# Weight ring of a mixture-of-experts layer: buffers laid out once, and the refill after the first round taken singly, into half a buffer

## Chip, cores and metric

The kernel runs on one core of a Trainium2 chip. The metric is the device time of one execution in microseconds (us); of several runs the median is given.

## The reference

One layer of an encoder on 512 tokens of width 1024, in float32. Three token mixers (neighbourhood attention, grouped-query attention, attention into 256 memory tokens) run on projections of the same input and are merged with gates; then comes a normalization, and then a feed-forward layer of 16 experts in which each expert chooses its 64 tokens:

```python
logits = jnp.einsum('btd,de->bte', x, w_router)
aff = jax.nn.softmax(logits, axis=-1)
gate, idx = lax.top_k(jnp.swapaxes(aff, 1, 2), cap)      # cap = 64
xs = x[bidx, idx]
h = jnp.einsum('becd,edf->becf', xs, w_gate_up)          # w_gate_up (16, 1024, 2048)
hg, hu = jnp.split(h, 2, axis=-1)
ye = jnp.einsum('becf,efd->becd', jax.nn.silu(hg) * hu, w_down)   # w_down (16, 1024, 1024)
...
return jnp.zeros_like(x).at[bidx, idx].add(ye)
```

A second normalization of `alpha * x + ffn` is the output. The experts' weights are 16 x 3 x 1024 x 1024 floats, 201 MB, and every one of them is needed.

## The kernel before

The program has two halves. In the first, TensorE works through the mixers' projections; their weights come through buffers of their own. In the second, the 16 experts follow one another. The instructions of each engine stand in the order in which the program writes them, and each engine waits for semaphores where it needs another's result.

The experts' weights are cut into 192 units of 128 rows by 2048 floats (1.05 MB, 8 KB in each of the 128 partitions). Expert `e` has eight units `("gu", e, k)` for the products `g` and `u` (function `gate_up`, line 1295) and four units `("dn", e, k)` for `y` (function `down`, line 1330; for the last expert `product`, line 1450). `_blocks` (lines 44 to 61) puts the units in the order of their use and deals them out in rounds to the twelve buffers of `RING`: ten hold a pair (16 KB in each partition), and `raw` and `VS` one unit. Three buffers serve only one or two rounds (`ROUNDS`), after which the kernel uses their space for results. The first round holds units 0 to 21.

The class `Ring` (lines 793 to 844) issues the transfers on SyncE's queue. `load` takes the next block, lays out a tile `w<number>` in its buffer and issues one DMA (line 817), or, for blocks that reach into the last `N_SINGLE` = 10 units, one for each unit (line 815). The first round is issued during the first half, as its buffers come free. After that `done`, which `gate_up`, `down` and `product` call behind the products of a unit, counts the units left in the block; when a block has been used up, the next block of the stream is issued. Since SyncE's queue keeps its order, an issue that waits holds those behind it. A DMA also waits until the eighth DMA before it has landed, since eight semaphores are taken in turn. In HBM the units lie in the order of the blocks (`_expert_rows`); the two units of a pair lie interleaved, so that a partition's 16 KB are one run.

While the tokens are being chosen the ring is full and no transfer is under way. Then `gather` collects the first two experts' tokens, and expert 0's eight `gu` units are used with a step of `gather` between them:

```python
if e == 0:
    for k in range(KD):
        gate_up(0, (k,))
        steps(g0)
```

Near the end, `ring.free_at_end` gives the tag of a buffer that no further block needs; its space takes parts of the sum `acc`.

Of the kernel before, what the change touches and what calls it, by code (L numbers as in the profile page):

```python
# [18 lines left out]
P = 128  # L19
D = 1024  # L20
# [11 lines left out]
RING = (("Q2", 2), ("Q1", 2), ("Q5", 2), ("Q7", 2), ("Q4", 2), ("Q3", 2), ("Q6", 2), ("raw", 1), ("Q9", 2), ("VS", 1),  # L32
        ("G1", 2), ("M", 2))
ROUNDS = {"raw": 1, "G1": 2, "VS": 2}
N_SINGLE = 10
X_SCALE = 1024.0
A_SCALE = 16384.0


def lead(e):  # L40
    return 2 if e == NEXP - 2 else 4


def _blocks():
    order = []
    for e in range(NEXP - 1):
        order += [("gu", e, k) for k in range(lead(e))]
        if e:
            order += [("dn", e - 1, k) for k in range(4)]
        order += [("gu", e, k) for k in range(lead(e), KD)]  # L50
    order += [("gu", NEXP - 1, k) for k in range(KD)]
    order += [("dn", e, k) for e in (NEXP - 2, NEXP - 1) for k in range(4)]
    blocks, i, r = [], 0, 0
    while i < len(order):
        for tag, n in RING:
            left = ROUNDS.get(tag, len(order)) - r
            if left > 0 and i < len(order):
                blocks.append((tag, n, order[i:i + n], i + n > len(order) - N_SINGLE, left > 1))
                i += n
        r += 1  # L60
    return blocks

# [2 lines left out]
def layer_kernel(ctx: ExitStack, tc: tile.TileContext, xt, xn, first0, wu, bgate, rpb, gains, wrt,  # L65
                 lnp, lnt, wx, csn, nmask, tri, iota, out, dbg=None):
    nc = tc.nc
# [12 lines left out]
    def R(tag, shape, name, dt=F32, bufs=None):  # L80
        return rp.tile(shape, dt, name=name, tag=tag, bufs=bufs)
# [55 lines left out]
    class Stream:  # L137
        AHEAD_DMA = 2

        def __init__(self):  # L140
            self.nd = 0
            self.ns = 0
            self.used = 0
            self.raw = {}
            self.hl = {}
# [121 lines left out]
    gT = cp.tile([P, KD], F32, name="gT")  # L267
    nc.gpsimd.tensor_scalar(gT, lnT[:, 0], 1.0 / X_SCALE, None, op0=ALU.mult)

# [523 lines left out]
    class Ring:  # L793
        def __init__(self):
            self.blocks = _blocks()
            self.at = {}
            self.row = [0]
            for b, (_, n, keys, _, _) in enumerate(self.blocks):
                self.row.append(self.row[-1] + P * n)
                for j, key in enumerate(keys):  # L800
                    self.at[key] = (b, j)
            self.n = 0
            self.left = [len(b[2]) for b in self.blocks]
            self.lent = len(RING)
            self.t = {}
            self.free_at_end = []

        def load(self):
            tag, n, keys, apart, _ = self.blocks[self.n]
            r0 = self.row[self.n]  # L810
            full = R(tag, [P, 2 * n, D], f"w{self.n}")
            src = wx[r0:r0 + P * len(keys)].rearrange("(p j) (h c) -> p (j h) c", j=len(keys), h=2)
            if apart:
                for j in range(len(keys)):
                    nc.sync.dma_start(full[:, 2 * j:2 * j + 2], src[:, 2 * j:2 * j + 2])
            else:
                nc.sync.dma_start(full[:, :2 * len(keys)], src)
            for j, key in enumerate(keys):
                t = [full[:, 2 * j + h] for h in range(2)]
                if key[0] == "dn" and key[1] == NEXP - 1:  # L820
                    t = [x.rearrange("p (c n) -> p c n", c=4) for x in t]
                self.t[key] = t
            self.n += 1

        def upto(self, n):
# [7 lines left out]
            return self.t.pop(key)  # L833

        def done(self, *key):
            b, _ = self.at[key]
            self.left[b] -= 1
            if self.left[b] == 0:
                tag, again = self.blocks[b][0], self.blocks[b][4]
                if again:  # L840
                    if self.lent >= len(self.blocks):
                        self.free_at_end.append(tag)
                    self.lent += 1
            self.upto(self.lent)

    ring = Ring()
    for i in range(4):
# [220 lines left out]
    def norm_cols(ms):  # L1068
        c = slice(ms[0], ms[-1] + 1)
        nc.gpsimd.tensor_scalar(r13[:, c], rs_y[:, c], X_SCALE, None, op0=ALU.mult)  # L1070
        for m in ms:
# [298 lines left out]
    def residual():  # L1370
        for h in range(2):
# [8 lines left out]
            for mp in range(2):  # L1380
                nc.vector.scalar_tensor_tensor(a[mp], a[mp], DN_ALPHA / X_SCALE, g, op0=ALU.mult, op1=ALU.mult)
                if mp == 0:
# [271 lines left out]
def _down_slots(w):  # L1654
    import numpy as np
    a = w.reshape(NEXP, 4, 2, 128, 1024).swapaxes(2, 3).reshape(NEXP, 4, 128, 2048).copy()
    a[-1] = w[-1].reshape(2, 4, 128, 4, 256).transpose(3, 2, 0, 1, 4).reshape(4, 128, 2048)
    return a


def _expert_rows(wgu, wdn):
    import numpy as np
    dn = _down_slots(wdn)
    unit = {"gu": lambda e, k: wgu[e, k * P:(k + 1) * P], "dn": lambda e, k: dn[e, k]}
    return np.concatenate([np.stack([unit[t](e, k) for t, e, k in keys], 1).reshape(-1, 2048) for _, _, keys, _, _ in _blocks()])


def _norm_rows(g1, b1, g2, b2):
# [17 lines left out]
def _prep(inp):  # L1686
# [51 lines left out]
    for ty in range(3):  # L1738
# [20 lines left out]
        "lnp": _norm_rows(*(np.asarray(inp[n])[0] for n in ("ln1_g", "ln1_b", "ln2_g", "ln2_b"))),  # L1759
        "lnt": np.stack([np.asarray(inp[n])[0].reshape(8, 128).T for n in ("ln1_g", "ln1_b")], 1),  # L1760
        "wx": _expert_rows(np.asarray(inp["w_gate_up"])[0], np.asarray(inp["w_down"])[0]),
        "csn": csn, "nmask": nmask, "tri": tri,
        "iota": np.broadcast_to(np.arange(1, 65, dtype=f), (128, 64)),
# [24 lines left out]
```

## Time and profile before

| what | value |
|---|---|
| median of 3 runs | 968.36 us (968.03 to 968.84) |
| the profiled execution | 967.9 us |
| its span in the profile | 966.1 us |
| TensorE busy in the span | 943.5 us (98%) |
| moved by DMA | 251.19 MB |
| ring DMAs by the page (2048 KB; 1024 KB) | 89; 14 |
| granted TensorE clock | 0.998 |

The profile is of one execution. Times in it count from the start of its span. TensorE's matmuls are pipelined and their ends are modelled, so that a share of 98% doesn't say that no matmul waited. PE is TensorE, ACT ScalarE, DVE VectorE, POOL GpSimd, SP SyncE; SPq is SyncE's sequencer, which issues the DMAs. `w<-in_wx` are the ring's transfers. A row of a window gives the busy time and the number of instructions of each engine, then the granted clock, the share of time in which the 16 DMA engines were busy, and the rate in GB/s.

### The profile page before, as it was taken

The numbers are of one execution on the slowest core, as the hardware profiler recorded it, in microseconds if no ns is written. First come the engines' busy times: TensorE is split into PE (matmuls) and PEld (weight loads), VectorE is DVE, ScalarE is ACT, GpSimd is POOL, SyncE is SP. The second block draws the span as 40 slices with busy tenths as digits, with TensorE's granted clock in tenths as the row PEclk, the third lists the DMA queues.
The fourth block names the chain that finished last, engine by engine and source line by source line (L and its number), as shares of the span: only waits on it lengthen the run. The fifth ranks groups of instructions, "written<-read, shape, count | busy, mean of one in ns | idle before, by whom it ended". The sixth has DMA issues, their size and how long they took to land.

```text
span 966.1 us, 13195 instructions
## 1 busy us (share of the span) xinstructions
PE 943.5 (98%) x5406; PEld 615.1 (64%) x5406; DVE 453.0 (47%) x851; ACT 277.2 (29%) x545; POOL 84.6 (9%) x98
## 2 busy tenths in 40 slices
PE   9999999999999999999999999999999999998996
PEld 9899878889888888887885333433343333532344
DVE  6347668874376566237464212653322222231426
ACT  5334454544354454323242111100010001100123
POOL 0102303000022231000023000000000000000003
PEclk9999999999999999999999999999999999999999
DMA  9321111211333322575919999999999999999992
GB/s 361 113 67 66 66 66 44 67 61 50 102 104 105 100 82 84 213 285 206 370 50 373 410 427 433 430 428 431 432 428 430 431 431 429 431 430 432 428 408 94
DMA packets 38329, 251.19 MB, mean 260 GB/s; under 512 B 12911, under 2 KB 13295, under 8 KB 24830
## 3 DMA queue, kind: packets, MB, share of 16 engines
q1 hardware_dynamic: 37550, 249.74, 63.9%
q8 instruction: 42, 0.69, 0.3%
q10 hardware_dynamic: 720, 0.62, 0.2%
q14 instruction: 17, 0.14, 0.0%
HBM read 247.46 MB, written 2.10 MB: 258 GB/s over the span
## 4 chain that ended last, share of the span: by engine, by line
PE 80%; DMA 10%; DVE 6%; ACT 1%; issue 1%; POOL 1%; DVEq 0%; POOLq 0%; ACTq 0%; SPq 0%
DMA w<-in_wx 10%; PE g L1295 10%; PE u L1295 9%; PE y L1330 8%; PE gate L274 4%; PE gate L275 4%; PE gate L276 4%; PE pr L274 2%; PE gy L649 2%; PE ga L1255 2%; PE pr L275 2%; PE pr L276 2%; PE nqk L274 2%; PE nqk L276 2%; PE nqk L275 2%; PE gt L636 1%
## 5 line engine op out<-in xcount | busy, mean ns | idle before, releaser
L1295 PE MATMUL g<-w,xs 128*64 128x512 f32 x512 | 135.1, 606 | 4.0 <-DMA w<-in_wx 3.9
L1295 PE MATMUL u<-w,xs 128*64 128x512 f32 x512 | 131.6, 592 | 0.0
L1330 PE MATMUL y<-w,hT 128*64 128x512 f32 x480 | 106.6, 594 | 3.4 <-DMA w<-in_wx 2.7
L93 DVE TENSOR_TENSOR y<-y,y 64x512 fp32r<-64x512 f32 x30 | 20.7, 689 | 134.5 <-ACT y L92 134.5
L1295 PEld LDWEIGHTS u<-w,xs 128*64 128x64 f32 x512 | 36.8, 137 | 73.1 <-issue 72.3
L92 ACT CAST y<-y 64x512 fp32r<-64x512 f32 x30 | 17.4, 580 | 224.9 <-PE y L1330 213.6
L1330 PEld LDWEIGHTS y<-w,hT 128*64 128x64 f32 x480 | 33.8, 137 | 72.1 <-issue 63.8
L93 DVE TENSOR_TENSOR los<-raw_twin,whi 128x1024 fp32r<-128x1024 f32 x43 | 54.1, 1259 | 52.5 <-ACT whi L92 52.2
L276 PE MATMUL gate<-xh,los 128*128 128x512 f32 x192 | 74.8, 390 | 0.0
L1295 PEld LDWEIGHTS g<-w,xs 128*64 128x64 f32 x512 | 30.5, 136 | 55.4 <-issue 43.9
L274 PE MATMUL gate<-xh,whi 128*128 128x512 f32 x160 | 63.5, 397 | 0.0
L275 PE MATMUL gate<-xl,whi 128*128 128x512 f32 x160 | 62.3, 390 | 0.0
L1402 DVE TENSOR_TENSOR acc<-acc,cb 128x512 f32<-128x512 f32 x56 | 35.6, 683 | 37.8 <-PE cb L1400 37.8
L92 ACT CAST whi<-raw_twin 128x1024 fp32r<-128x1024 f32 x43 | 45.1, 1049 | 8.3 <-PE wo L1093 4.4
L1471 POOL TENSOR_TENSOR acc<-acc,ln2g 128x512 f32<-128x512 f32 x6 | 7.6, 1280 | 431.4 <-DVE l2s L1499 429.4
L93 DVE TENSOR_TENSOR los<-raw_twin,los 128x1024 fp32r<-128x1024 f32 x21 | 26.5, 1263 | 35.2 <-ACT los L92 35.1
L276 PEld LDWEIGHTS gate<-xh,los 128*128 128x128 f32 x192 | 36.0, 188 | 7.8
L625 ACT ACTIVATE att_twin<-gs,nm 128x512 f32<-128x512 f32 x32 | 21.7, 684 | 51.1 <-DVE nm L624 51.1
L1305 ACT ACTIVATE tg<-g 128x512 f32<-128x512 f32 x16 | 9.5, 597 | 90.5 <-PE g L1295 90.5
L274 PEld LDWEIGHTS gate<-xh,whi 128*128 128x128 f32 x160 | 30.0, 188 | 7.1 <-issue 1.2
L275 PEld LDWEIGHTS gate<-xl,whi 128*128 128x128 f32 x160 | 30.1, 188 | 5.9
L1318 DVE COPY hT<-ht 128x512 f32<-128x512 f32 x15 | 10.3, 690 | 44.4 <-PE ht L1313 44.4
(432 smaller groups left out, 1893.8 us busy)
## 6 DMA issues: line engine op xcount, KB each, us to landing
w<-in_wx SPq DMA_DIRECT2D x89, 2048.0 KB
raw_twin<-in_wu SPq DMA_DIRECT2D x65, 512.0 KB
w<-in_wx SPq DMA_DIRECT2D x14, 1024.0 KB
raw<-in_wu SPq DMA_DIRECT2D x8, 512.0 KB
xr<-in_xt SPq DMA_DIRECT2D x4, 512.0 KB
macc<-in_xn SPq DMA_DIRECT2D x2, 1024.0 KB
first<-in_first SPq DMA_DIRECT2D x4, 384.0 KB
bf<-in_rpb SPq DMA_DIRECT2D x64, 24.0 KB
```

The costliest lines, as they stand in the source:

```text
L92: nc.scalar.copy(hi, src)
L93: nc.vector.tensor_tensor(lo, src, hi.bitcast(F32), op=ALU.subtract)
L274: nc.tensor.matmul(acc, w_h, rh[:, k], start=(k == 0), stop=False)
L275: nc.tensor.matmul(acc, w_h, rl[:, k], start=False, stop=False)
L276: nc.tensor.matmul(acc, w_l, rh[:, k], start=False, stop=(k == nk - 1))
L625: nc.scalar.activation(self.p[:, h], self.s[h], AF.Exp, bias=nm[:, h:h + 1], accum_out=self.sm[:, h:h + 1])
L649: nc.tensor.matmul(self.y[h * 64:h * 64 + 64, :P], ST["vg"][:, kc, kvh * 64:kvh * 64 + 64], self.pt[:, h, kc], start=(kc == 0), stop=(kc = ...
L1255: nc.tensor.matmul(g, XH[:, m, c], oh[:, m, sl], start=(m == 0), stop=False)
L1295: nc.tensor.matmul(GU[e][b][hf * 64:hf * 64 + 64], xs, w[b][:, hf * 512:hf * 512 + 512], start=(k == 0), stop=(k == KD - 1))
L1318: nc.vector.tensor_copy(t, tp)
L1330: nc.tensor.matmul(y[o * 64:o * 64 + 64], hT[:, c, hf * 64:hf * 64 + 64], w[j][:, o * 512:(o + 1) * 512], start=(k == 0 and j == 0), stop= ...
L1402: nc.vector.tensor_tensor(a, a, cb, op=ALU.add)
```

## The change

Each buffer of the ring is laid out once, at its first block, and kept (`home`); later blocks are written to the same tile or to half of it. `_blocks` now deals out, for each block that is not in the first round, either the pair or two blocks of one unit each, which have a half number `h`. Single are the blocks that end before unit `FULL` = 36 of the stream, which comes to units 22 to 33 (the pair of units 34 and 35 ends at 36 and stays a pair), and, as before, the last ones (units 181 to 191). `done` marks a half as no longer busy and issues the next blocks of the stream as long as the halves they need are not busy. The order of the stream, and the buffer of each unit, stay. Units that are single now lie in HBM as a run of 8 KB in each partition; the last ones lay interleaved in pairs before. `free_at_end` names the same buffer.

In numbers: 109 ring DMAs instead of 103; twelve transfers of 1.05 MB stand in the place of six of 2.1 MB. On SyncE each single waits for TensorE by itself, and on TensorE the first product of each of these units waits for its own transfer.

```diff
 N_SINGLE = 10
+FULL = 36
...
-                blocks.append((tag, n, order[i:i + n], i + n > len(order) - N_SINGLE, left > 1))
+                keys = order[i:i + n]
                 i += n
+                if r and (i < FULL or i > len(order) - N_SINGLE):
+                    blocks += [(tag, h, [key]) for h, key in enumerate(keys)]
+                else:
+                    blocks.append((tag, 0, keys))
...
         def load(self):
-            tag, n, keys, apart, _ = self.blocks[self.n]
-            r0 = self.row[self.n]
-            full = R(tag, [P, 2 * n, D], f"w{self.n}")
-            src = wx[r0:r0 + P * len(keys)].rearrange("(p j) (h c) -> p (j h) c", j=len(keys), h=2)
-            if apart:
-                for j in range(len(keys)):
-                    nc.sync.dma_start(full[:, 2 * j:2 * j + 2], src[:, 2 * j:2 * j + 2])
-            else:
-                nc.sync.dma_start(full[:, :2 * len(keys)], src)
+            tag, h, keys = self.blocks[self.n]
+            n = len(keys)
+            src = wx[self.row:self.row + P * n].rearrange("(p j) (h c) -> p (j h) c", j=n, h=2)
+            if tag not in self.home:
+                self.home[tag] = R(tag, [P, 2 * dict(RING)[tag], D], f"w{self.n}")
+            full = self.home[tag][:, 2 * h:2 * (h + n)]
+            nc.sync.dma_start(full, src)
...
         def done(self, *key):
-            b, _ = self.at[key]
-            self.left[b] -= 1
-            if self.left[b] == 0:
-                tag, again = self.blocks[b][0], self.blocks[b][4]
-                if again:
-                    if self.lent >= len(self.blocks):
-                        self.free_at_end.append(tag)
-                    self.lent += 1
-            self.upto(self.lent)
+            tag, h = self.at[key]
+            self.busy.discard((tag, h))
+            if self.n == len(self.blocks):
+                if not self.busy & {(tag, 0), (tag, 1)}:
+                    self.free_at_end.append(tag)
+                return
+            while self.n < len(self.blocks):
+                tag, h, keys = self.blocks[self.n]
+                if self.busy & {(tag, h + j) for j in range(len(keys))}:
+                    break
+                self.load()
```

More of the change, by code (lines that the diff above doesn't have):

```diff
@@ L795, in __init__ @@
             self.blocks = _blocks()
[L796 to L805, printed above, removed]
+            self.n = self.row = 0
+            self.t, self.at, self.home = {}, {}, {}
+            self.busy = set()
             self.free_at_end = []
         def load(self):
-            tag, n, keys, apart, _ = self.blocks[self.n]
-            r0 = self.row[self.n]
-            full = R(tag, [P, 2 * n, D], f"w{self.n}")
-            src = wx[r0:r0 + P * len(keys)].rearrange("(p j) (h c) -> p (j h) c", j=len(keys), h=2)
-            if apart:
-                for j in range(len(keys)):
-                    nc.sync.dma_start(full[:, 2 * j:2 * j + 2], src[:, 2 * j:2 * j + 2])
-            else:
-                nc.sync.dma_start(full[:, :2 * len(keys)], src)
+            tag, h, keys = self.blocks[self.n]
[5 more added lines that the diff above has]
+            nc.sync.dma_start(full, src)
             for j, key in enumerate(keys):
-                t = [full[:, 2 * j + h] for h in range(2)]
+                t = [full[:, 2 * j + i] for i in range(2)]
                 if key[0] == "dn" and key[1] == NEXP - 1:
@@ L822, in load @@
                 self.t[key] = t
+                self.at[key] = (tag, h + j)
+                self.busy.add((tag, h + j))
+            self.row += P * n
             self.n += 1
@@ L1664, in _expert_rows @@
     unit = {"gu": lambda e, k: wgu[e, k * P:(k + 1) * P], "dn": lambda e, k: dn[e, k]}
-    return np.concatenate([np.stack([unit[t](e, k) for t, e, k in keys], 1).reshape(-1, 2048) for _, _, keys, _, _ in _blocks()])
+    return np.concatenate([np.stack([unit[t](e, k) for t, e, k in keys], 1).reshape(-1, 2048) for _, _, keys in _blocks()])
 def _norm_rows(g1, b1, g2, b2):
```

## Prediction

> **What bounds the kernel now.** I read the page first, then the chain that ended last, then TensorE's waits, then the transfer rates in small windows. From the page, the span and the two rows on DMA in 40 slices of 24.15 us:
>
> ```profile
> span 966.1 us, 13195 instructions
> DMA  9321111211333322575919999999999999999992
> GB/s 361 113 67 66 66 66 44 67 61 50 102 104 105 100 82 84 213 285 206 370 50 373 410 427 433 430 428 431 432 428 430 431 431 429 431 430 432 428 408 94
> ```
>
> The slice at 483 to 507 us moves 50 GB/s: the ring is full and nobody uses it up yet. From the next slice on the DMA engines are busy to the end of the weights. The chain that ended last, at its late end:
>
> ```profile
> 842.85 35.30 DMA w<-in_wx
> 878.21 38.84 DMA w<-in_wx
> 917.08 19.61 DMA w<-in_wx
> 936.82 1.98 PE yq L1450 x32
> ```
>
> So the last stage starts when a weight unit lands at 936.8, and from there to the end of the span lie 29.3 us of products and the second normalization, which the change does not touch. TensorE meets the transfers late and briefly (total, times, longest; then the first three such waits):
>
> ```profile
> PE g L1295 <- DMA w<-in_wx: 3.9, 5, 1.2
> PE y L1330 <- DMA w<-in_wx: 2.7, 3, 1.2
> PE yq L1450 <- DMA w<-in_wx: 0.6, 1, 0.6
> ```
> ```profile
> 873.33 1.08 PE L1295 MATMUL g<-w,xs 128*64 128x512 f32 x4 [0.51 <-DMA w<-in_wx]
> 878.19 1.08 PE L1295 MATMUL g<-w,xs 128*64 128x512 f32 x4 [1.21 <-DMA w<-in_wx]
> 883.06 1.08 PE L1295 MATMUL g<-w,xs 128*64 128x512 f32 x4 [0.62 <-DMA w<-in_wx]
> ```
>
> Hence the ring's lead lasts until 873 us, and then the stream of transfers sets the time. If the stream comes g earlier, TensorE still reaches the first wait when it did; the three waits take up 0.51 + 1.21 + 0.62 = 2.34 us, and all waits together 7.2 us. A g of up to 2.3 us has passed to TensorE whole by 883 us, and up to 7.2 us could. What counts is therefore where the stream loses time between the restart and the end (window, busy time and count of each engine, clock, DMA share, GB/s):
>
> ```profile
> 522.00:525.00 3.00, 3.00 (x22) 1.03 (x18) 0.00 (x0) 0.46 (x1) 0.00 (x0) 1.00 0.57 186
> 525.00:529.00 4.00, 4.00 (x30) 1.72 (x30) 0.41 (x1) 0.46 (x1) 0.00 (x0) 1.00 1.01 422
> 529.00:531.00 2.00, 2.00 (x16) 0.79 (x14) 0.17 (x1) 0.00 (x0) 0.00 (x0) 1.00 0.97 360
> 531.00:534.00 3.00, 3.00 (x20) 1.08 (x18) 0.30 (x2) 0.66 (x2) 0.00 (x0) 1.00 0.97 404
> 534.00:536.00 2.00, 2.00 (x14) 0.65 (x12) 1.06 (x6) 0.30 (x1) 0.00 (x0) 1.00 1.00 295
> 536.00:540.00 4.00, 4.00 (x26) 1.51 (x24) 2.02 (x4) 0.60 (x1) 0.00 (x0) 1.00 0.94 393
> 540.00:545.00 5.00, 5.00 (x36) 2.10 (x34) 0.69 (x2) 0.46 (x1) 0.00 (x0) 1.00 1.00 423
> 600.00:800.00 200.00, 199.25 (x980) 79.19 (x980) 73.67 (x122) 20.92 (x36) 0.00 (x0) 1.00 1.01 430
> ```
>
> Against the steady 430 GB/s the first seven windows lack 732 + 32 + 140 + 78 + 270 + 148 + 35 = 1435 KB, which is 3.34 us of stream. Half of it (1.70 us) is the hole at 522 to 525; the rest lies at the hand-offs from one pair to the next. After 545 nothing is missing.
>
> **The change part by part.** First, the release. The issues of the pairs on SyncE's queue, and TensorE's last products of the first two units:
>
> ```profile
> 515.54 0.33 SPq L817 DMA_DIRECT2D w<-in_wx  x1
> 523.02 0.33 SPq L817 DMA_DIRECT2D w<-in_wx  x1
> 527.86 0.33 SPq L817 DMA_DIRECT2D w<-in_wx  x1
> 532.70 0.33 SPq L817 DMA_DIRECT2D w<-in_wx  x1
> 537.17 0.33 SPq L817 DMA_DIRECT2D w<-in_wx  x1
> ```
> ```profile
> 519.53 1.03 PE L1295 MATMUL u<-w,xs 128*64 128x512 f32 x4
> 521.95 1.03 PE L1295 MATMUL u<-w,xs 128*64 128x512 f32 x4
> ```
>
> The pair issued at 523.02 waited for the second unit, done at 522.98. The new kernel waits for the first unit alone, done at 520.56, so unit 22 goes out at about 520.6, which is 2.4 us sooner, and each next one a unit's time (2.42 us) later; a unit takes 1.049 MB / 430 = 2.44 us. Supply and release thus run at the same pace until TensorE quickens (the pair after 532.70 came 4.47 us later, not 4.84).
>
> Whether that closes the hole depends on what is queued at each issue. Bytes issued less bytes moved, from these rows:
>
> ```profile
> 520.60:523.50 2.90, 2.90 (x26) 1.31 (x24) 0.41 (x1) 0.00 (x0) 0.00 (x0) 1.00 0.67 277
> 523.50:532.70 9.20, 9.20 (x59) 3.36 (x59) 0.82 (x2) 0.92 (x2) 0.00 (x0) 1.00 0.94 369
> 523.50:537.17 13.67, 13.67 (x87) 5.12 (x88) 2.33 (x10) 2.47 (x6) 0.00 (x0) 1.00 0.96 363
> 523.50:550.73 27.23, 27.23 (x171) 10.38 (x172) 5.06 (x14) 3.39 (x8) 0.00 (x0) 1.00 0.97 392
> 523.50:556.36 32.86, 32.86 (x199) 12.06 (x199) 5.99 (x16) 4.81 (x11) 0.00 (x0) 1.00 0.98 399
> ```
>
> At 520.6 the pair of 515.54 still has 2.90 x 277 = 803 KB to go, 1.87 us of work. Unit 22 can follow it without a hole: the 1.70 us go. At 532.70 before, 2 pairs (4.19 MB) were issued and 3.39 MB moved: 1.9 us queued, and the hand-off behind it (534 to 536) lost 0.63 us. The hand-off at 529 to 531 lost 0.33. At 537.17, with 3 pairs issued and 4.96 MB moved, 3.1 us were queued, and 540 to 545 lost 0.08. So a hand-off with under 2 us queued costs 0.3 to 0.6 us, and with 3.1 us nearly nothing.
>
> The singles begin at 1.87 us. What a hand-off loses stays in the queue, since the issues come from TensorE's pace; so the losses stop when the queue has grown from 1.87 to 3.1 us, or earlier when TensorE quickens after 533. They cost 0 to 1.2 us in all. I take one hand-off like each of the two rows, 0.33 + 0.63 = 0.96 us.
>
> Second, the size. Twelve units in eight-kilobyte rows instead of six pairs in sixteen. The nearest rows are the last eleven singles, which the kernel before already has, and the end of the stream:
>
> ```profile
> 900.00:940.00 40.00, 38.69 (x196) 14.85 (x194) 15.15 (x26) 8.16 (x15) 0.00 (x0) 1.00 1.00 425
> 940.00:943.50 3.50, 3.27 (x42) 2.90 (x44) 0.78 (x4) 0.52 (x2) 0.00 (x0) 1.00 0.41 173
> ```
>
> 425 against 430 GB/s is 1.2% of 12 x 2.44 = 29.3 us: 0.35 us. Bounds: 0, and 0.7 were all of that window's deficit due to the half of it that are singles. The rule that speaks against this part is the Trainium skill's, DMA: Bandwidth & Descriptors, section "Anatomy of one DMA": a fixed cost of about 2.0 us for each DMA (fitted on GpSimd's path). By it, six more DMAs with nothing behind which to hide would be an estimated 12 us; the row of 425 GB/s with a full queue disagrees for queued singles, and no row shows singles on a short queue.
>
> Third, the last ten units. They were already issued singly, two per released buffer; now each goes when its own half is free. There SyncE waits for earlier transfers to land and not for TensorE, so the issue times stay; cover is the queue itself. Their source rows are now contiguous, where they lay at twice their length before: worth between 0 and, by the same 425 against 430 over those 25 us, 0.3 us. I take 0.
>
> Fourth, SyncE and the other queues. Six more issues of 0.33 us lie in its idle time between releases. A waiting issue holds only later ring issues, since all else on SyncE before the output is ahead of it. The buffers laid out once give the same addresses and the same stream order; ACT, DVE and POOL wait for other transfers than before at a few places, transfers of earlier rounds of the ring. TensorE waits once per unit instead of once per pair, in a stretch in which the rows above show it no wait on a transfer (the first is at 873 us): nothing.
>
> Fifth, what is late next. The first pair after the singles was issued at 550.73 with 6 pairs out (12.58 MB) and 10.67 MB moved: 4.4 us queued; the next at 556.36 with 14.68 MB out and 13.11 moved: 3.65 us. A stream that is 2.0 us ahead finds 2.4 and 1.65 us there, again in the range of losing hand-offs: 0 to 0.9 us more. I take 0, because the stream's end is set by the last of 16 engines (the taper at 940 to 943.5 us, share 0.41), which has more queued than the mean; the 0.9 stays for the range.
>
> The sum: 3.34 - 0.96 - 0.35 = 2.03 us off the stream and off the end. The profiled execution took 967.9 us around its span of 966.1 and would take 965.9; it lay 0.46 us under the median of the three runs (968.36), so the median goes to 966.3 us. About 0.2% (1.94 us) is what a measurement of this kernel can tell from no change, so the forecast lies just past that edge.
>
> **The rivals.** (a) The hole closes, but the gain is spent again: hand-offs cost the full 1.2 us, and the two pairs at 550 and 556 us 0.9 us more. 3.34 - 1.2 - 0.35 - 0.9 = 0.9 us: 967.5. For it speaks that 1.65 us queued is just where pairs lost time; against it, that the slowest engine is not the one that runs dry.
> (b) The end follows one slow engine, not the mean rate. The taper shows 3.5 us between first and last engine; if the last one was never idle at 522 to 525, it gains only its hand-offs. At worst nothing: 968.4. Against: 186 GB/s in that window is 43% of the rate, too little for most engines to have had work.
> (c) Slower: a single on a short queue pays its start whether or not the queue grows, a mechanism per DMA. The three hand-offs before lost 3.34 - 1.70 = 1.64 us, 0.55 each; twelve would lose 6.6, with 0.35 for size 6.9 against 3.34 now: 3.6 us later, 972.0. It decides from (3.34 - 0.35) / 12 = 0.25 us each. Against: in the rows the loss fell as the queue grew. The Trainium skill's rule above (DMA: Bandwidth & Descriptors, "Anatomy of one DMA") points the same way as (c); only the row of 425 GB/s speaks on it here, and against it.
> (d) The hand-offs cost nothing once the stream never stops: 3.34 - 0.35 = 3.0 us, 965.4.
> (e) The change doesn't do what it says, a half waiting for the whole buffer: no gain, 968.4. The instruction order shows a wait on TensorE of its own at every single, so I give it little.
>
> **How the numbers follow.** Forecast 0.44, (d) 0.18, (a) 0.14, (b) and (e) 0.10 together, (c) 0.14. Faster by over 0.2% are (d) and some three quarters of the forecast's own spread (1.8 to 2.4 us, as the hand-offs cost 0.6 to 1.2): 0.18 + 0.34 = 0.52. Within 0.2%: the rest of the forecast (0.10), (a), (b) and (e): 0.34. Slower: (c), 0.14. The range runs from (d) with the 0.3 us of the contiguous tail, 965.1, to (b) with the spread of the runs, 968.6, and leaves out (c).
>
> **What would show it.** Right: the first single issued near 520.6; no window near 523 under 300 GB/s; the bytes moved by 545 larger by some 0.85 MB; the unit for the last products landing near 934.7 and the rest of the span after it still 29.3 us. TensorE's waits on transfers should fall by about 2 us. Wrong: rates of 300 GB/s throughout 523 to 550 (c); a restored hole at 551 or 557 (a); more bytes by 545 but the landing still at 936.8 (b); a first single at 523.0 (e).

## The result, and the profile after

The kernel after takes 966.82 us (median of 22 runs), the kernel before 968.12 us (22 runs): a ratio of 0.9986, 95% interval 0.998 to 0.9992, so 1.3 us faster (0.8 to 1.9). The forecast was 966.3 us in a range from 965.1 to 968.6. The gain is real, since the interval excludes 1, but smaller than the 2.03 us of the sum, and below the 0.2% from which the prediction called it faster. The profiled execution took 966.57 us around a span of 964.7 us, 1.4 us less than the span before.

The release came as worked out. The first two singles on SyncE's queue, from the kernel after:

```profile
520.70 0.33 SPq L813 DMA_DIRECT2D w<-in_wx  x1
523.12 0.33 SPq L813 DMA_DIRECT2D w<-in_wx  x1
```

Then the stream, in the windows that the prediction summed for the kernel before (window, busy time and count of each engine, clock, DMA share, GB/s):

```profile
522.00:525.00 3.00, 3.00 (x22) 1.08 (x18) 0.00 (x0) 0.46 (x1) 0.00 (x0) 1.00 0.90 306
525.00:529.00 4.00, 4.00 (x32) 1.70 (x30) 0.41 (x1) 0.46 (x1) 0.00 (x0) 1.00 0.98 373
529.00:531.00 2.00, 2.00 (x18) 0.80 (x16) 0.07 (x1) 0.00 (x0) 0.00 (x0) 1.00 1.02 430
531.00:534.00 3.00, 3.00 (x20) 1.09 (x20) 0.34 (x1) 0.66 (x2) 0.00 (x0) 1.00 1.02 431
534.00:536.00 2.00, 2.00 (x14) 0.65 (x12) 1.05 (x6) 0.31 (x2) 0.00 (x0) 1.00 1.00 418
536.00:540.00 4.00, 4.00 (x26) 1.46 (x24) 2.08 (x5) 0.60 (x1) 0.00 (x0) 1.00 1.01 424
540.00:545.00 5.00, 5.00 (x38) 2.15 (x36) 0.59 (x2) 0.46 (x1) 0.00 (x0) 1.00 1.02 429
```

The hole of 186 GB/s is a dent of 306, and the hand-offs from 529 on lose next to nothing. Against 430 GB/s the windows lack 372 + 228 + 0 - 3 + 24 + 24 + 5 = 650 KB, 1.51 us of stream, where the kernel before lacked 3.34. Nearly all of it (1.40 us) now lies at one place, 522 to 529 us.

Two longer stretches, first of the kernel before, then of the kernel after:

```profile
517.00:545.00 28.00, 27.94 (x187) 11.20 (x187) 6.89 (x24) 3.39 (x8) 0.00 (x0) 1.00 0.92 365
555.00:570.00 15.00, 15.00 (x96) 5.62 (x91) 4.21 (x11) 2.57 (x5) 0.00 (x0) 1.00 1.00 427
517.00:575.00 58.00, 57.94 (x357) 22.10 (x357) 12.43 (x36) 7.00 (x15) 0.00 (x0) 1.00 0.97 399
```
```profile
517.00:545.00 28.00, 27.94 (x188) 11.20 (x188) 6.89 (x24) 3.39 (x8) 0.00 (x0) 1.00 0.98 394
555.00:570.00 15.00, 15.00 (x96) 5.71 (x92) 4.30 (x11) 2.57 (x5) 0.00 (x0) 1.00 1.00 415
517.00:575.00 58.00, 57.94 (x358) 22.06 (x358) 12.52 (x36) 6.99 (x15) 0.00 (x0) 1.00 1.00 409
600.00:800.00 200.00, 199.25 (x980) 79.16 (x980) 73.55 (x122) 20.90 (x36) 0.00 (x0) 1.00 1.01 430
```

By 545 us the new stream is (394 - 365) x 28 = 0.81 MB ahead, 1.89 us at 430 GB/s. By 575 us only (409 - 399) x 58 / 430 = 1.35 us are left. The loss between is in the window in which the first pairs behind the singles are handed over: 415 against 427 GB/s over 15 us is 0.42 us. From there the rate is the old 430.

The late end of the chain that ended last, and TensorE's waits on transfers (total, times, longest), of the kernel after:

```profile
876.51 39.05 DMA w<-in_wx
915.62 19.52 DMA w<-in_wx
935.28 1.98 PE yq L1451 x32
```
```profile
PE y L1331 <- DMA w<-in_wx: 2.6, 3, 1.2
PE g L1296 <- DMA w<-in_wx: 2.4, 3, 1.2
PE yq L1451 <- DMA w<-in_wx: 0.6, 1, 0.6
```

The unit for the last products lands at 935.28 instead of 936.82, 1.54 us sooner, and the rest of the span still takes 29.4 us. The waits fall from 7.2 to 5.6 us: the 3.9 us at the `g` products became 2.4. So the lead of 1.35 us at 575 arrived at the end, within what two single executions can tell. What such a landing is made of is told below, under "Mean engine and slowest engine" and "The passing to the end".

### The profile page after: what moved, and what is told of

The parts are those of the page before. It is cut to its first block, busy times and chain, and to the rows that moved or that the text cites. A ratio compares the mean times of both kernels' runs of the same rounds, so it can differ in the third digit from the quotient of the medians.

```text
span 964.7 us, 13206 instructions
## 1 busy us (share of the span) xinstructions
PE 943.4 (98%) x5406; PEld 615.4 (64%) x5406; DVE 452.3 (47%) x851; ACT 277.0 (29%) x545; POOL 85.5 (9%) x98
## 4 chain that ended last, share of the span: by engine, by line
PE 80%; DMA 10%; DVE 6%; ACT 1%; issue 1%; POOL 1%; DVEq 0%; POOLq 0%; ACTq 0%; SPq 0%
DMA w<-in_wx 10%; PE g L1296 10%; PE u L1296 9%; PE y L1331 8%; PE gate L279 4%; PE gate L281 4%; PE gate L280 4%; PE pr L279 2%; PE gy L654 2%; PE ga L1256 2%; PE pr L280 2%; PE pr L281 2%; PE nqk L279 2%; PE nqk L280 2%; PE nqk L281 2%; PE gt L641 1%
```

## The experiments

All ratios are to the kernel before on the same chip; the ratio on record is not the quotient of the two medians and differs from it by up to 0.0008. In what follows "lead at 575" is the rate of 517 to 575 us less the 399 GB/s of the kernel before, times 58 us, over 430 GB/s; it is 1.35 us in the profiled kernel after.

**Which part of the change does it.** The first four kernels differ from the kernel after in the constant `FULL` alone.

```diff
-FULL = 36
+FULL = 0      # only the last units single
```

> The new ring code with no early singles: units 22 to 35 come in pairs again, the last eleven units stay single and lie contiguous. Theory 1 (the early singles are the whole gain): the hole at 522 to 525 us is back at under 200 GB/s, time as the kernel before, 0 within 0.4 us. Rival (the contiguous, half-by-half tail brings part of it): 0.3 to 0.5 us faster than before, and a higher rate at 900 to 940 us than 425 GB/s.

Measured 968.67 against 968.57 us, ratio 0.9999 (0.9991 to 1.0008). The hole and the tail in this kernel:

```profile
522.00:525.00 3.00, 3.00 (x22) 1.17 (x20) 0.09 (x1) 0.46 (x1) 0.00 (x0) 1.00 0.71 235
900.00:930.00 30.00, 29.64 (x132) 10.75 (x130) 11.74 (x19) 5.82 (x10) 0.00 (x0) 1.00 1.00 426
```

The kernels before and after have 426 GB/s at 900 to 930 too. The layout of the buffers and the changed tail are worth nothing that can be measured (the interval is -0.9 to +0.8 us); the gain comes with the early singles. (The hole showed 235 GB/s and not the expected value under 200; the lead at 575 is still -0.1 us, at 398 GB/s.)

```diff
-FULL = 36
+FULL = 25     # only units 22 and 23 single
```

> Only units 22 and 23 come singly, all later early ones in pairs. If closing the hole behind the first round were all that matters: 1.3 us faster than before, as with twelve singles. If the later singles matter because a pair waits for two units on a short queue: a new hole in front of the pair of units 24 and 25, near 528 us, and 0.3 to 0.8 us faster than before.

Measured 967.69 against 968.57 us, 0.9994 (0.9985 to 1.0003). In the trace:

```profile
522.00:525.00 3.00, 3.00 (x22) 1.08 (x18) 0.00 (x0) 0.46 (x1) 0.00 (x0) 1.00 0.92 303
525.00:529.00 4.00, 4.00 (x32) 1.61 (x30) 0.41 (x1) 0.41 (x1) 0.00 (x0) 1.00 0.90 340
529.00:531.00 2.00, 2.00 (x18) 0.80 (x16) 0.00 (x0) 0.05 (x1) 0.00 (x0) 1.00 1.07 356
534.00:536.00 2.00, 2.00 (x14) 0.64 (x12) 0.96 (x6) 0.40 (x2) 0.00 (x0) 1.00 0.90 311
```

The first hole closes as in the kernel after (303 against 306), but each pair behind it loses at its own hand-off, since it is still issued a unit's time late. The lead at 575 is 0.1 us (400 GB/s). The hole moved on and was not removed.

```diff
-FULL = 36
+FULL = 44     # singles up to unit 42
```

> Singles go on to unit 42 (the whole second round) instead of unit 33. Theory 1 (the lead of 1.9 us of stream that the new kernel has at 545 us is spent at 556 to 572 us because the pairs of units 34 to 42 are released late onto a short queue): the lead at 575 us stays near 1.9 us or grows, time 2.0 to 2.6 us under the kernel before. Theory 2 (the lead goes to a stall of one DMA engine that has nothing to do with the release): 1.3 us, as the new kernel. Theory 3 (each single costs rate): 0.2 to 0.3 us worse than the new kernel.

Measured 966.72 against 968.57 us, 0.9984 (0.9975 to 0.9993).

```profile
555.00:570.00 15.00, 15.00 (x95) 5.67 (x92) 4.43 (x11) 2.57 (x5) 0.00 (x0) 1.00 1.01 425
517.00:575.00 58.00, 57.94 (x357) 22.07 (x357) 12.66 (x36) 7.00 (x15) 0.00 (x0) 1.00 1.00 410
```

With more singles the rate at 555 to 570 is back at 425, against 415 in the first execution of the kernel after, so the loss there goes with the late pairs (how much it varies is shown below). The lead at 575 is 1.5 us. The gain of 1.5 us (0.7 to 2.4) stayed under the expected 2.0 to 2.6 and can't be told from that of the kernel after.

```diff
-FULL = 36
+FULL = 200    # every unit behind the first round single
```

> Every unit after the first round comes singly, 170 transfers of 1.05 MB. If a single costs the 0.03 us that the prediction took for its size: some 148 more of them than in the new kernel make 4.4 us, so 3 us slower than before. If singles cost nothing on a filled queue: as with singles to unit 42, 2.0 to 2.6 us faster than before, at 430 GB/s between 600 and 800 us.

Measured 970.03 against 968.57 us, 1.0013 (1.0003 to 1.0022): slower.

```profile
600.00:800.00 200.00, 199.25 (x980) 79.11 (x980) 73.66 (x122) 20.92 (x36) 0.00 (x0) 1.00 1.01 426
517.00:575.00 58.00, 57.94 (x358) 22.06 (x358) 12.54 (x36) 7.00 (x15) 0.00 (x0) 1.00 1.00 411
```

This measures a single by itself, with a full queue: 426 against 430 GB/s, 0.93% of 2.44 us, 0.023 us each. The page lists 172 DMAs of 1024 KB here and 34 in the kernel with singles up to unit 42; 138 x 0.023 = 3.2 us, and the medians of the two differ by 970.03 - 966.72 = 3.3 us. So stream time goes into the end one to one, and with a full queue a single's price is far below the 0.25 us from which rival (c) decided; (c) is about a short queue, which comes below. The twelve singles of the change cost 0.27 us.

The Trainium skill's rule (DMA: Bandwidth & Descriptors, "Anatomy of one DMA") of about 2.0 us fixed for each DMA, fitted for DMAs that GpSimd issues, would make 138 more of them an estimated 276 us, were nothing to hide it; here 3.3 us were paid, so that for these queued DMAs of SyncE all but about 1% of it is hidden.

**Why the hand-off at 522 to 529 still loses 1.4 us.** The prediction held that a hand-off's loss depends on what is queued when it comes. The next kernels bring units in two halves of 0.52 MB: the ring's unit has a half `w[0]` (read by the products with `b == 0`) and a half `w[1]`, and the first half of the next unit goes out as soon as the `b == 0` products are done. Units before `HALF` come so.

```diff
+HALF = 23
...
-                    blocks += [(tag, h, [key]) for h, key in enumerate(keys)]
+                    for h, key in enumerate(keys):
+                        parts = (0, 1) if i - len(keys) + h < HALF else (None,)
+                        blocks += [(tag, h, [key], b) for b in parts]
...
+            part = slice(0, 2 * n) if b is None else slice(b, b + 1)
-            nc.sync.dma_start(full, src)
+            nc.sync.dma_start(full[:, part], src[:, part])
...
+                if b == 0:
+                    ring.part("gu", e, k)
```

> The new kernel, but unit 22 comes in two transfers of 0.52 MB, the first as soon as the gate half of unit 0 has been used, about 0.9 us sooner. Theory 1 (what a hand-off loses depends on how much is queued when the next transfer is issued): some 2.7 us are queued then instead of 1.9; the windows 522 to 525 and 525 to 529, which lack 0.87 and 0.53 us of stream in the new kernel, lack less than half of that; 0.5 to 0.8 us faster than the new kernel, 1.8 to 2.2 us under the kernel before. Theory 2 (each transfer that starts on a short queue pays, whatever is queued): the same or 0.2 to 0.4 us slower than the new kernel.

Measured 967.0 against 968.1 us, 0.9986 (0.9977 to 0.9995).

```profile
520.02 1.19 SPq L817 DMA_DIRECT2D w<-in_wx  x2
```
```profile
522.00:525.00 3.00, 3.00 (x20) 1.08 (x18) 0.00 (x0) 0.46 (x1) 0.00 (x0) 1.00 0.82 276
525.00:529.00 4.00, 4.00 (x30) 1.58 (x28) 0.41 (x1) 0.31 (x1) 0.00 (x0) 1.00 1.03 393
```

The first half went out at 520.02, 0.68 us sooner, with more left in the queue; the two windows lack 462 + 148 = 610 KB, 1.42 us against 1.40 in the kernel after, and the time is the same. The dependence on the queue, by which the prediction sized this term, did not show. Over the traces of the kernels here those two windows lack 1.1 to 1.5 us in the seven executions with six or more singles and none in halves, 1.4 in this one, and 1.9 us in the three with four or twelve units in halves.

```diff
-FULL = 36
+FULL = 44
+HALF = 26     # units 22 to 25 in halves
```

> Units 22 to 25 in halves, singles to unit 42: eight transfers of 0.52 MB, then seventeen of 1.05 MB. Theory 1: as the kernel with only unit 22 halved or 0.2 us better, 2.0 to 2.4 us under the kernel before. Theory 2: every half pays 0.3 us, so 1 us slower than the new kernel.

Measured 968.14 against 968.1 us, 1.0004 (0.9994 to 1.0013): the gain is gone. By the medians it is 1.1 us behind the two other kernels with halves on the same chip, and its eleven runs lie further apart than the eleven of any other version, from 967.18 to 970.89 us. The lead at 575 was nevertheless 1.2 us (408 GB/s) in its profiled execution, at 967.18 us the fastest of its 11 runs.

```diff
+HALF = 34     # units 22 to 33 in halves
```

> All twelve early singles (units 22 to 33) in halves, 24 transfers of 0.52 MB. Theory 1: the queue is no shorter than with only unit 22 halved, so the same time as that kernel, less 0.3 to 0.5 us for the smaller rows (12 units at twice the 0.02 us that a single costs). Theory 2: 2 to 3 us slower than the new kernel.

Measured 967.04 against 968.1 us, 0.9987 (0.9978 to 0.9996).

```profile
522.00:525.00 3.00, 3.00 (x22) 1.15 (x20) 0.00 (x0) 0.46 (x1) 0.00 (x0) 1.00 0.74 257
525.00:529.00 4.00, 4.00 (x30) 1.58 (x28) 0.41 (x1) 0.18 (x1) 0.00 (x0) 1.00 0.99 356
```

Here 24 transfers stand in the place of the twelve singles, and the time is that of the kernel after. A start paid by each transfer on a short queue, rival (c), is refuted: at its 0.25 us, twelve more transfers would have cost 3 us. What is lost at 522 to 529 (519 + 296 KB, 1.9 us) is lost near the restart, whether the transfers behind it are 12, 13 or 24.

```diff
-FULL = 36
+FULL = 30     # the pair of units 28 and 29 ends at 30 and stays a pair
```

> Singles end at unit 29 instead of 33; units 30 to 33 come in pairs at a time when TensorE is quicker and the queue longer. If the queue at each issue decides: the pair of units 30 and 31 is released at 541.4 us, with some 2.4 us queued, and loses 0.1 to 0.4 us; 0.9 to 1.3 us faster than before. If the number of singles decides: half the gain of twelve or less, 0.6 us.

The last single is unit 27 (the page lists 20 DMAs of 1024 KB, six more than the kernel before). Measured 967.93 against 968.1 us, 0.9995 (0.9986 to 1.0004).

```profile
536.00:540.00 4.00, 4.00 (x26) 1.43 (x24) 1.84 (x3) 0.60 (x1) 0.00 (x0) 1.00 1.00 385
540.00:545.00 5.00, 5.00 (x38) 2.18 (x36) 1.00 (x2) 0.46 (x1) 0.00 (x0) 1.00 0.98 354
```

The first pairs behind the singles lose 180 + 380 = 560 KB, 1.3 us, at their hand-offs; the lead at 575 is 0.7 us (404 GB/s). The pairs that follow the singles of the kernel after lose 0.42 us in its first execution. So in these traces pairs that begin later lose less.

**Whether the stream sets the end.** One unit of the stream, 1.05 MB, is not fetched; the products with it use what the buffer held before.

```diff
-            nc.sync.dma_start(full, src)
+            m = 2 if ("dn", 7, 2) in keys else 2 * n
+            nc.sync.dma_start(full[:, :m], src[:, :m])
```

> The new kernel without the transfer of one unit in the middle of the stream (the third down unit of expert 7, near 715 us): TensorE does the same products on what the buffer held before, so the output of that expert is not the layer's. If the stream of transfers sets the end one to one: 2.4 us faster than the new kernel (the time of 1.05 MB at 430 GB/s), 3.5 to 3.9 us under the kernel before, and the end of the waits of TensorE on transfers moves by as much. If the end hangs on something else as well (TensorE's own work, the slow one of the DMA engines in another way): under 1.5 us faster than the new kernel.

Measured 963.95 against 968.58 us, 0.996 (0.9947 to 0.9972). The end of the chain in this kernel:

```profile
913.00 19.56 DMA w<-in_wx
932.70 1.98 PE yq L1452 x32
```

On the same chip the kernel after had 0.9985 (its second measurement, below). The difference of 0.0025 is 2.4 us, which is one unit at 430 GB/s, 2.44 us; with intervals of about 1.2 and 0.9 us on either side it is not finer than that, and by the medians themselves the difference is 967.18 - 963.95 = 3.2 us. Even 3.9 us of stream below the kernel before still reach the end: nothing else takes over as the bound there.

**The four halves once more.** To see whether the loss with four halved units came from the halves or from the singles up to unit 42:

```diff
+HALF = 26     # as above, but FULL = 36 as in the kernel after
```

> Units 22 to 25 in halves and units 26 to 33 single, pairs from unit 34. With only unit 22 halved, and with all twelve halved, the time was that of the new kernel (0.9986 and 0.9987 of before); with four halved and singles to unit 42 it was 1.0004. If halves cost nothing and that run was set by what one DMA engine met by chance: 1.0 to 1.5 us faster than before. If four halves followed by singles do cost something: within 0.5 us of before.

Measured 967.85 against 968.58 us, 0.9996 (0.9987 to 1.0004); 407 GB/s in 517 to 575. By the ratio that is less gain than with none, one or twelve units in halves, but the interval overlaps theirs (0.9976 to 0.9994 for the kernel after on this chip), so that a loss is shown only for the kernel with singles up to unit 42. The trace shows a lead of 1.1 us at 575, and the next part shows that the stream as a whole lost nothing to the halves; what came late was its slowest engine.

**Both good versions again, on the same chip.**

> The new kernel once more, on one chip with the version with singles to unit 42, so that the two can be set side by side: 1.3 us faster than before. Its bytes moved between 517 and 575 us should again be some 10 GB/s over the kernel before.

> Singles to unit 42 once more, beside the new kernel. If the loss at 555 to 570 us that it takes away (0.4 us of stream) reaches the end, less 0.2 us for nine more singles: 0.2 us faster than the new kernel. If the end is set by one engine's chance: the same or either way by up to 0.5 us.

The kernel after measured 967.18, the one with singles up to unit 42 967.0, against 968.58 us: 0.9985 (0.9976 to 0.9994) and 0.9987 (0.9978 to 0.9996). No version beats the kernel after by what can be measured. In this execution of the kernel after, the late end of the chain reads:

```profile
916.38 19.56 DMA w<-in_wx
936.08 1.98 PE yq L1451 x32
```

The same kernel lands the same unit at 935.28 in one execution and at 936.08 in another, so a landing in a single trace carries some 0.8 us of spread. The rates vary as well: this execution has 407 GB/s at 517 to 575 and 423 at 555 to 570, the earlier one 409 and 415.

**Mean engine and slowest engine.** A transfer is shared by 16 DMA engines, and the trace holds 16 semaphore events for its landing, read here as one from each engine. The mean of the 16 tells where the stream is ("the mean engine" below); the last one tells when the transfer is complete. For the last unit of the stream the mean, counted from the issue of units 20 and 21, was 426.28 us in the kernel before and 424.97 and 424.99 us in the two executions of the kernel after: 1.31 and 1.29 us sooner. With the tail alone it was 426.19. So in this measure executions of a like stream agree within 0.15 us, much closer than their times. The last of the 16 events comes behind that mean by 1.5 to 3.2 us in the fourteen traces (before 2.21, after 1.86 and 2.09), and the issue itself moves by up to 1.0 us from one execution to the next. The 0.8 us between the two executions of the kernel after are 0.54 us of later issue (516.16 instead of 515.62) and 0.23 of the slowest engine.

The kernels with four units in halves are, by the mean engine, 1.33 us (singles up to unit 42) and 1.25 us (up to 33) ahead of the kernel before, and the one with twelve 1.29: no loss to the halves. In the traced execution of the kernel with four halved and singles up to 33, the slowest engine is 2.94 us behind the mean at the end, and lands unit 42 at 580.2 us, just as in the kernel before (580.2). Whether the halves make an engine late, or it came so by chance, one trace of each kernel can't tell.

## Why the prediction was right, and where it was not

**The release.** Forecast 520.6, measured 520.70. Right.

**The hole.** It was to go whole. What was left after the change at 522 to 545 us, 1.51 us, was forecast as 0.96 for the hand-offs and 0.35 for size, 1.31 together. The sum is near by luck, for its explanation fell. The prediction let the loss at a hand-off fall from 0.6 us to nothing as the queue grew from 1.9 to 3.1 us. The first unit in halves gave the queue 0.68 us more and lost the same 1.4 us; twelve units in halves lost no time either. No window near 523 under 300 GB/s was expected, and 306 was found; but the dent reaches to 529. With small transfers behind it the loss is paid once, near the restart, and not by the rule that the 0.96 us were taken from. By the semaphore events of the trace, the first of the 16 DMA engines ends the pair ahead of the singles (units 20 and 21) at 522.7 us and the last at 525.3, so some engines are done well before others, as in the taper at the end that the prediction quoted. But for the most part the engines did not stand idle: their busy share is 0.90 and 0.98 in the two windows, against 1.01 in the steady stretch, so idleness accounts for 0.11 x 3 + 0.03 x 4 = 0.45 of the 1.40 us. The rest was lost while they worked: by the trace's records of single packets, those of 8 KB took up to 1.45 us there, with a median of 0.31. The rows from which the prediction read its rule say the same: 529 to 531 and 534 to 536 have 360 and 295 GB/s at shares of 0.97 and 1.00. So a queue run dry is the smaller part of what a hand-off loses; why packets are slow behind a restart stays open.

**The size.** Forecast 0.35, measured 12 x 0.023 = 0.27 us by the kernel of singles throughout. Right. Rival (c), the dearest, fell with the result and with the kernel of 24 halves on the short queue.

**The tail.** Forecast 0; the kernel with this part alone gives 0.9999. Right.

**What is late next.** This is the term that was mis-sized. The pairs issued behind the singles were put at 0, with a bound of 0.9 us, because the slowest engine was to set the end. They lost 0.42 us at 555 to 570 in the first trace (415 against 427), 0.14 in the second (423), and 0.07 with the singles continued (425). The loss goes with the lead that the stream has when they come, as it would if a stream further ahead finds less queued there; that reason was not tested by itself. The six executions in which the pairs begin at unit 34, with the lead at 545 us (the rate of 517 to 545 us less 365 GB/s, times 28 us, over 430 GB/s):

| execution | lead at 545, us | GB/s at 555 to 570 |
|---|---|---|
| unit 22 in halves | 1.95 | 399 |
| kernel after, first | 1.89 | 415 |
| one unit left out (later, near 715 us) | 1.89 | 412 |
| kernel after, second | 1.56 | 423 |
| four units in halves, singles up to 33 | 1.17 | 426 |
| twelve units in halves | 1.17 | 430 |

The argument from the slowest engine gave no cover. On the mean engine, counted from the issue of units 20 and 21, the kernel after is 2.0 and 1.9 us ahead of the kernel before at unit 33, and 1.3 and 1.4 at unit 42 (its two executions). The slowest engine follows that only loosely: it lands unit 33 at 555.1 and 557.5 us instead of 558.4, and unit 42 at 578.7 and 579.4 instead of 580.2, so that it lost 1.8 us of its lead in the one execution and next to nothing in the other.

**The passing to the end.** The gain was to reach the end whole. The landing moved by 1.54 us, TensorE's waits fell by 1.6 us, the span by 1.4, the medians by 1.3; and 2.44 us less stream gave 2.4 us less time by the ratios (3.2 by the medians, 2.2 on the mean engine). Right, though the first trace of the kernel after had some luck: its last unit landed 1.58 us sooner, of which 1.31 are the mean engine's and 0.35 a slowest engine that was less late behind it, less 0.08 for a later issue.

By the measured terms the sum is 3.34 - 1.51 - 0.42 = 1.41 us. The forecast of 2.03 was 0.2 us short of the loss at the restart and 0.4 short of that at the late pairs. So what happened lies between the forecast and rival (a), whose mechanism (the gain partly spent again at the pairs behind the singles) took place at about half its price at the pairs (0.42 of 0.9). (d) is out, as hand-offs still cost; (c) is out, as said; (b) is out as the whole, since the gain is there, though its mechanism is seen: the slowest engine sets the end and scatters the times, but it gains with the others; (e) is out by 520.70. Of the chances, that of faster by over 0.2% was too high: it took as certain that the spread of the forecast hangs on the hand-offs alone, and left out the late pairs, which were bounded in the text at 0.9 us and would by that have put most of the forecast's own spread below the edge.

Over the kernels that differ in `FULL` alone, the lead at 575, the end of the stream on the mean engine and the time go together (where a kernel was run twice, the traces are of both):

| singles up to unit | lead at 575 us | last unit on the mean engine, against before | change of time by the ratio |
|---|---|---|---|
| none (tail only) | -0.1 | -0.1 | -0.1 (interval -0.9 to +0.8) |
| 23 | 0.1 | -0.3 | -0.6 (-1.5 to +0.3) |
| 27 | 0.7 | -0.6 | -0.5 (-1.4 to +0.4) |
| 33 (kernel after) | 1.35; 1.1 | -1.3; -1.3 | -1.4 (-1.9 to -0.8) |
| 42 | 1.5; 1.5 | -1.6; -1.5 | -1.5 (-2.4 to -0.7) |
| all | 1.6, then 0.023 per single | +1.25 | +1.3 (+0.3 to +2.1) |

## What to carry to other kernels

Where a full prefetch ring stops and restarts, a buffer given back in pieces closes the hole only if the pieces go on for long enough; else the hole moves to the first large transfer behind them. Here two single units brought 0.3 us by the mean engine, six 0.6, twelve 1.3 and twenty-one 1.5 to 1.6. Small transfers cost little while the queue is full (0.023 us for each of 1.05 MB here), but over a whole stream that is more than the hole is worth, so they belong only where the queue is short. Before passing a gain on, look at the queue at the first transfer after the changed stretch: what was late enough to be harmless before comes nearer by just the gain. And where a gain is smaller than the scatter of the times, the mean of the engines' landing events, counted from the restart, can show it more sharply than the time does.

## What the runs showed of the hardware

- With a full queue, transfers of 1.05 MB in rows of 8 KB run at 426 GB/s and pairs in rows of 16 KB at 430.
- At a restart on about 2 us of queued work, some 1.1 to 1.9 us of stream were lost, for the most part while the engines were busy (0.90 and 0.98 of the two windows in the kernel after), and neither a first issue 0.68 us sooner nor twelve units in halves changed the time. The cause is open.
- The 16 engines of one stream end apart: the last was 1.5 to 3.2 us behind the mean at the end of the stream, not the same amount in two executions of one kernel.
- With four units in halves one kernel lost the gain (1.0004, where one or twelve units in halves have 0.9986 and 0.9987), and a second may have (0.9996, with an overlapping interval). The mean engine lost nothing in either trace. This is not explained.
